# One-bank accumulator tiles and a new order at the end of a stage, in a two-block transformer kernel

## The chip, the cores and the metric

The kernel runs on one core of a Trainium2 chip. The metric is the device time of one execution in microseconds (us), as the median of three runs. The work is done by TensorE (PE; its weight loads are shown apart as PEld), VectorE (DVE), ScalarE (ACT) and GpSimd (POOL); SyncE (SP) issues most of the DMAs.

## The reference

The input is one sequence of 256 tokens with 1024 features in fp32. A first block has two layers, a second block has one. Cut to what matters here:

```python
def first_block(x, ...):                       # two layers
    for layer in range(2):
        f = swiglu(rms_norm(x, g[0]), w_ffn_gate, w_ffn_up, w_ffn_down)   # d_ff = 2816
        x = x + 0.5 * rms_norm(f, g[1])
        h = rms_norm(x, g[2])
        m = short_conv_mixer(h, ...) if layer == 0 else diff_attention(h, k, v, ...)
        x = x + rms_norm(m, g[3])
        f = swiglu(rms_norm(x, g[4]), ...)
        x = x + 0.5 * rms_norm(f, g[5])
        if layer == 0:
            k, v = shared_kv(x, g_kv, w_kv)

def second_block(x, ...):                      # one layer
    proj = rmsnorm(x, norm1_g) @ w_in
    y_a = hgrn2_mixer(...); y_b = nsa_mixer(...)
    merged = g_a * (y_a @ w_br_a) + g_b * (y_b @ w_br_b)
    h = x + merged @ w_out
    h = h + square(relu(rmsnorm(h, norm2_g) @ w_ff1)) @ w_ff2             # d_ff = 4096
    return rmsnorm(h, final_g)
```

## The kernel before

**Precision and weights.** Every large product is made of three fp32r matmuls: each operand is split into a rounded part and a remainder, and high by high, low by high and high by low are added up in PSUM. The weights are streamed from HBM in chunks of two pieces (128 x 1024 each) through three raw buffers. `Stream.hi` (L162) makes the rounded part of the next piece on ACT (L171, tile `wh`), `Stream.lo` (L175) makes its remainder on DVE (L181, tile `wl`) and then calls `load`, which issues the DMA for a further chunk on SP (L148) when a raw buffer has been used up. There are ten slots for split pieces: `hi` does nothing when the slot ten pieces back has not been given back by `done`, and nothing when the raw chunk may not be loaded yet. `pump` is one `hi` and one `lo`.

**Stages.** The 256 tokens are two blocks of 128 (`tb` 0 and 1). A stage begins with `stage_ab` (or, for the attention and for the second block, with `section`s): it multiplies block 0 and then block 1 of the normed, transposed input by the first pieces of the stage's weights. Its input is `XT`: `fill(tb)` makes eight transposes on PE into two PSUM tiles `tr` (L385), and ACT and DVE copy them out as rounded part `xth` (L389) and remainder `xtl` (L390); for one stage they lie in tiles `h` instead (L395, L396). `fill(1)` stands inside `stage_ab`, ahead of the last quarter of block 0's work.

**The end of a stage.** The kernel has eight stage ends, each a `Tail`: ends 1, 3, 4 and 6 close the four gated FFNs, end 2 the convolution, end 5 the attention's output projection, end 7 the merge of the second block's two mixers, and end 8 the last FFN and with it the kernel. `lead` adds rows 0 to n-2 of block 0; `close` adds the last row of block 0, then the rows of block 1. A row is 6 matmuls of 512 columns into two accumulators. After a block's last row comes its norm, in four steps: `c1` reads the two accumulators on ACT (squares, L287) and DVE (L309, or L303 where there is no norm on the output) and starts a root on POOL (L298); `c2` adds to the residual `x` (L320) and takes squares again; `c3a` multiplies by the next gain (L334) and starts the second root; `c3b` scales (L338). Then the block can be transposed by `fill`.

**Order.** Inside `with ordered():` the instructions of PE, ACT, DVE and POOL are each kept in the order in which they are written; outside of it a scheduler orders them. Every engine works through its own queue in that order, so an instruction that waits holds up all behind it on its engine. In `close` the splits of the next stage's pieces (`st.hi`, `st.lo`), the norm steps, the rows and `fill(0)` are interleaved by hand.

**PSUM.** There are eight banks of 512 fp32 columns. The tags `mm` and `tr` have two tiles of one bank each. The tag `acc` has two tiles of two banks each: `new_acc` gives block 0 the first bank and block 1 the second bank of each tile. The attention scores (`att_scores`, two score maps of a head) and the scores of the second block (`nsa_scores`, two branches) take one such tile, one map or branch to a bank.

Of the kernel before, what the change touches and what calls it, by code (L numbers as in the profile page):

```python
# [209 lines left out]
def tile_model(ctx: ExitStack, tc: tile.TileContext, w, wkv, x_in, gains, cst_in, pos_in, lbp, out):  # L210
# [10 lines left out]

    def ps(tag, n=512):
        uid[0] += 1
        return psum.tile([P, n], F32, name=f"{tag}_{uid[0]}", tag=tag)

# [194 lines left out]
    def new_acc():  # L420
        t = [ps("acc", D).rearrange("p (t c) -> p t c", t=2) for _ in range(2)]
        return lambda tb, n: t[n][:, tb]

# [28 lines left out]
    @contextmanager  # L452
    def ordered():
        order.mark(False)
        yield
        order.mark(True)
# [86 lines left out]
    class Tail:  # L543
# [19 lines left out]
        def close(self, at=None, ahead=0):  # L563


            bd, n = self.bd, self.n
            at = n - 1 if at is None else at
            with ordered():
                for i in range(at, n):
                    self.row(0, i)  # L570
                rows = list(range(ahead, n - 1))
                for i in rows[:2]:
                    self.row(1, i)
                st.hi()
                bd.c2(0)
                bd.c3a(0)
                st.hi()
                st.lo()
                bd.c3b(0)
                for i in rows[2:4]:  # L580
                    self.row(1, i)
                    st.hi()
                    st.lo()
                for i in rows[4:]:
                    self.row(1, i)
                    st.hi()
                st.lo()
                bd.fill(0)
                self.row(1, n - 1)
                st.hi()  # L590
                st.lo()
                bd.c2(1)
                bd.c3a(1)
                st.lo()
                bd.c3b(1)
                while st.lo():
                    pass
# [120 lines left out]
    st.load()  # L718
    g0b = [ps("acc", D)[:, :512] for _ in range(2)]
    for n in range(2):  # L720
# [117 lines left out]
    def att_scores(h, kq):  # L838
        sc = ps("acc", D).rearrange("p (c k) -> p c k", c=2)
        for c in range(2):  # L840
            r = slice(c * 64, c * 64 + 64)
            mm(sc[:, c, 0:256], kq[r, 1, P:], kq[r, 0], True, True)
            mm(sc[:, c, 256:384], kq[r, 1, :P], kq[r, 0, :P], True, True)
        return sc

    def att_soft(h, sc):
        ev = sb([P, D], "ev", bufs=2)
        dg = sc[:, :, 128:384].rearrange("p c (a k) -> p c a k", a=2)
        nc.vector.tensor_tensor(dg, dg, negm[:, None, None, :].to_broadcast([P, 2, 2, P]), op=OP.add)
        nm = sb([P, 4], "nm", bufs=2)  # L850
        p = ev[:, :768].rearrange("p (c k) -> p c k", c=2)
        sm = sb([P, 4], "sm", bufs=2)
        spans = (slice(0, 256), slice(256, 384))
        for i, sp in enumerate(spans):
            nc.vector.tensor_reduce(nm[:, 2 * i:2 * i + 2], sc[:, :, sp], axis=AX.X, op=OP.max, negate=True)
        for i, sp in enumerate(spans):
            for c in range(2):
                q = 2 * i + c
                nc.scalar.activation(p[:, c, sp], sc[:, c, sp], AF.Exp, bias=nm[:, q:q + 1], accum_out=sm[:, q:q + 1])
        r = sb([P, 4], "smr", bufs=2)  # L860
        nc.vector.reciprocal(r, sm)
        rl = sb([P, 4], "rl", bufs=2)
        nc.vector.tensor_scalar(rl, r, neglam, None, op0=OP.mult)
        at = sb([P, D], "tmp", bufs=2)
        for i, sp in enumerate(spans):
            nc.vector.tensor_scalar(p[:, 1, sp], p[:, 1, sp], rl[:, 2 * i + 1:2 * i + 2], None, op0=OP.mult)
            nc.vector.scalar_tensor_tensor(at[:, sp], p[:, 0, sp], r[:, 2 * i:2 * i + 1], p[:, 1, sp],
                                           op0=OP.mult, op1=OP.add)
        return at
# [57 lines left out]
    def acc(tb, n):  # L927
        if tb and not acc1:
            acc1.extend(ps("acc", D)[:, :512] for _ in range(2))
        return (acc0, acc1)[tb][n]  # L930
# [241 lines left out]
    def nsa_scores(i):  # L1172
# [4 lines left out]
        cs = slice(tb * P, (tb + 1) * P)  # L1177
        sc = ps("acc", D).rearrange("p (b c) -> p b c", b=2)
        for b_ in range(2):
# [142 lines left out]
    def hg_sums(tb):  # L1322
# [3 lines left out]
        mm(o2, up, af[:, tb], True, True)  # L1326
        od = ps("acc", D)
        for h in range(4):
# [19 lines left out]
    def hg_attn(tb):  # L1348
# [4 lines left out]
        for c in range(2 - tb):  # L1353
            o = hv(ps("acc", D)[:, :512])
            r = slice(c * 64, c * 64 + 64)
# [77 lines left out]
    ya_h, ya_l = sb([P, KD, T], "xth", F32R)[:, :4], sb([P, KD, T], "xtl", F32R)[:, :4]  # L1433
    ob = [ps("acc", D).rearrange("p (m t) -> p m t", m=4) for _ in range(2)]
    for m in range(KD):
        ws_piece(ob[m // 4][:, m % 4], brs[m // 2], m % 2, YX(yb_h, yb_l, 4), range(4, 8))
        nc.vector.tensor_tensor(mgs[m][:, 1], mgs[m][:, 1], ob[m // 4][:, m % 4], op=OP.mult)
    ms = []
# [153 lines left out]
```

## Time and profile before

| | |
|---|---|
| median of 3 runs | 1455.8 us (1452.35 to 1456.35) |
| the profiled execution, its own time | 1455.11 us |
| its span, first to last instruction | 1453.3 us |
| PE busy | 1411.6 us, 97% of the span |
| DVE busy, ACT busy | 884.2 us (61%), 741.5 us (51%) |
| mean granted TensorE clock | 0.996 |

The median is 0.7 us over the time of the profiled execution, which is 1.8 us over its span. The views used below are: the busy times of the engines; the table of who waited for whom; the instructions of one engine in order of time, where a bracket at the end of a row gives the idle time of the engine before that row and what ended it; the chain that ended last, in which neighbouring pieces of the same kind are merged; and the groups of instructions by line, with their shapes. A matmul's duration in these rows overlaps that of the next one; the distance between two starts is what it costs.

### The profile page before, as it was taken

Reading aid. Unit: us, or ns where it says so; the run is one execution under the profiler, and the core shown is the slowest. Engines: PE = TensorE matmul, PEld = TensorE weight load, DVE = VectorE, ACT = ScalarE, POOL = GpSimd, SP = SyncE. Lnnn points to the kernel's source line nnn. Section 1 sums busy time; section 2 is a strip of 40 time slices with the busy share of each in tenths; the row PEclk is TensorE's granted clock in tenths of the full one; section 3 lists DMA queues with packets and bytes.
Section 4 is the critical chain, followed back from the end, with each engine's and each line's share of the span. In section 5 each row is a group of like instructions: output and inputs, shape, how many; then the busy total and the mean of one; then the engine's idle time right before and its main releaser. Section 6 shows DMA issues by size and latency. Waiting matters only on the chain.

```text
span 1453.3 us, 23106 instructions
## 1 busy us (share of the span) xinstructions
PE 1411.6 (97%) x9556; PEld 1288.2 (89%) x9556; DVE 884.2 (61%) x1332; ACT 741.5 (51%) x1212; POOL 48.7 (3%) x56
## 2 busy tenths in 40 slices
PE   7999999999999999999999999999999998999997
PEld 6999979979999799998798799997887898899995
DVE  5565566866555475654776765554878556665552
ACT  5454454445444444543665554444575864464451
POOL 0000000010000000000100100000000000000000
PEclk9999999999999999999999999999999999999999
DMA  7554546446554355554343465543653233455530
GB/s 271 206 210 175 193 168 217 155 171 225 185 192 174 145 206 201 187 182 167 147 172 131 160 232 187 191 168 126 232 189 116 98 148 135 146 200 196 184 143 29
DMA packets 37801, 252.93 MB, mean 174 GB/s; under 512 B 4288, under 2 KB 4672, under 8 KB 8896
## 3 DMA queue, kind: packets, MB, share of 16 engines
q1 hardware_dynamic: 36656, 250.20, 47.4%
q8 instruction: 75, 1.23, 0.3%
q10 hardware_dynamic: 1008, 1.25, 0.2%
q14 instruction: 30, 0.25, 0.0%
q0 software_dynamic: 32, 0.00, 0.0%
HBM read 250.39 MB, written 1.05 MB: 173 GB/s over the span
## 4 chain that ended last, share of the span: by engine, by line
PE 87%; DVE 5%; DMA 2%; ACT 2%; issue 2%; POOL 1%; POOLq 0%; DVEq 0%; ACTq 0%
PE mm L399 58%; PE acc L399 25%; PE tr L399 2%; DMA raw<-in_w_dram 2%; DVE wl L181 2%; POOL ssr L298 1%; ACT junk L287 1%; ACT wh L171 1%; DVE x L320 1%; PE tr L385 1%; PE tr L521 0%; PE tr L1203 0%; DVE tmp L309 0%; DVE xtl L390 0%; DMA gain<-in_gains_dram 0%
## 5 line engine op out<-in xcount | busy, mean ns | idle before, releaser
L181 DVE TENSOR_TENSOR wl<-raw,wh 128x1024 fp32r<-128x1024 f32 (+1 forms) x460 | 550.3, 1219 | 188.6 <-ACT wh L171 185.3
L171 ACT ACTIVATE wh<-raw 128x1024 fp32r<-128x1024 f32 (+1 forms) x460 | 473.1, 1050 | 187.5 <-PE mm L399 92.8
L399 PE MATMUL mm<-xth,wh 128*128 128x256 f32 x1728 | 490.7, 284 | 3.6 <-DVE ev L1449 3.6
L399 PE MATMUL mm<-xtl,wh 128*128 128x256 f32 x1728 | 488.5, 283 | 0.0
L399 PE MATMUL mm<-xth,wl 128*128 128x256 f32 x1728 | 486.1, 281 | 0.0
L399 PE MATMUL acc<-wh,h 128*128 128x512 f32 x1120 | 354.3, 397 | 3.8 <-DVE tmp L309 3.2
L399 PEld LDWEIGHTS mm<-xth,wh 128*128 128x128 f32 x1728 | 324.2, 188 | 6.5 <-DVE ev L1449 4.2
L399 PEld LDWEIGHTS mm<-xth,wl 128*128 128x128 f32 x1728 | 327.1, 189 | 0.6 <-issue 0.5
L399 PEld LDWEIGHTS mm<-xtl,wh 128*128 128x128 f32 x1728 | 325.0, 188 | 2.1 <-issue 0.5
L399 PEld LDWEIGHTS acc<-wh,h 128*128 128x128 f32 x1120 | 205.8, 188 | 53.4 <-DVE tmp L309 5.3
L399 PE MATMUL acc<-wl,h 128*128 128x512 f32 x560 | 221.3, 395 | 0.0
L399 PE MATMUL mm<-wh,xth 128*128 128x256 f32 (+2 forms) x496 | 159.2, 321 | 7.9 <-ACT xth L389 7.9
L399 PE MATMUL mm<-wh,xtl 128*128 128x256 f32 (+2 forms) x496 | 158.3, 319 | 4.1 <-DVE xtl L390 4.0
L399 PE MATMUL mm<-wl,xth 128*128 128x256 f32 (+2 forms) x496 | 157.2, 317 | 0.0
L399 PEld LDWEIGHTS acc<-wl,h 128*128 128x128 f32 x560 | 105.2, 188 | 25.4
L527 ACT ACTIVATE ev<-mm 128x256 f32<-128x256 f32 x74 | 28.4, 384 | 166.4 <-PE mm L399 165.1
L399 PEld LDWEIGHTS mm<-wh,xth 128*128 128x128 f32 x496 | 96.0, 194 | 14.8 <-ACT xth L389 10.6
L399 PEld LDWEIGHTS mm<-wh,xtl 128*128 128x128 f32 x496 | 96.2, 194 | 10.2 <-DVE xtl L390 6.1
L399 PEld LDWEIGHTS mm<-wl,xth 128*128 128x128 f32 x496 | 96.1, 194 | 4.6
L528 DVE TENSOR_TENSOR ev<-ev,mm 128x256 f32<-128x256 f32 x74 | 31.2, 421 | 99.0 <-ACT ev L527 99.0
L427 ACT ACTIVATE h<-ev 128x256 fp32r<-128x256 f32 x114 | 47.4, 418 | 81.9 <-DVE ev L528 38.0
L428 DVE TENSOR_TENSOR h<-ev,h 128x256 fp32r<-128x256 f32 x114 | 48.2, 425 | 51.8 <-ACT h L427 51.8
(276 smaller groups left out, 960.2 us busy)
## 6 DMA issues: line engine op xcount, KB each, us to landing
raw<-in_w_dram SPq DMA_DIRECT2D x225, 1024.0 KB, 4.8
gain<-in_gains_dram SPq DMA_DIRECT2D x15, 512.0 KB, 3.8
raw<-in_wkv_dram SPq DMA_DIRECT2D x4, 792.0 KB, 4.7
x<-in_x_dram SPq DMA_DIRECT2D x2, 512.0 KB, 5.4
raw<-in_w_dram SPq DMA_DIRECT2D x2, 512.0 KB, 5.6
ev<-in_lbp_dram SPq DMA_DIRECT2D x1, 512.0 KB, 5.8
out_dram<-tmp ACTq DMA_DIRECT2D x2, 256.0 KB, 2.8
out_dram<-tmp SPq DMA_DIRECT2D x2, 256.0 KB, 2.6
```

The costliest lines, as they stand in the source:

```text
L171: self.nc.scalar.activation(h, r, AF.Copy)
L181: self.nc.vector.tensor_tensor(l, r, h.bitcast(F32), op=OP.subtract)
L287: nc.scalar.activation(junk, src, AF.Square, accum_out=self.ss[key][:, n:n + 1])
L298: nc.gpsimd.tensor_tensor(self.r[key], v[:, 1:2], half[:, :1], op=OP.pow)
L320: nc.vector.scalar_tensor_tensor(x[:, tb, c], self.t[tb][:, c], r, x[:, tb, c], op0=OP.mult, op1=OP.add)
L385: nc.tensor.transpose(pt[:, j * P:(j + 1) * P], xn[:, k * P:(k + 1) * P], ident)
L399: nc.tensor.matmul(o, lhsT=a, rhs=b, start=start, stop=stop)
L427: last["act"] = nc.scalar.activation(dst[:, 0], src, AF.Copy).ins
L428: last["dve"] = nc.vector.tensor_tensor(dst[:, 1], src, dst[:, 0].bitcast(F32), op=OP.subtract).ins
L527: nc.scalar.activation(s, o[:, 0], AF.Silu)
L528: nc.vector.tensor_tensor(hf, s, o[:, 1], op=OP.mult)
```

## The change

1. All accumulators become tiles of one bank: `ps` loses its width, and the tag `acc` gets four tiles of one bank in place of two of two banks. `new_acc` gives each of its four accumulators (2 blocks x 2 halves) a tile of its own. The tiles that used only a part of two banks (`g0b`, `acc1`, the sums of `hg_sums`, the products of `hg_attn`) shrink to one bank. The four pairs of the merge (`ob`) lie in four tiles in place of two.
2. `att_scores` gives each of the two score maps a tile of its own, and `att_soft` handles them one after the other: the mask is added in two instructions of 256 columns in place of one of 512, and the maximum is taken in four instructions (256 and 128 columns for each map) in place of two.
3. `nsa_scores` puts both branches into one bank (256 columns each), with four such tiles in flight in place of two.
4. `close` has a new order. `c3b(0)` follows `c3a(0)` directly, with no split between. Only four `hi` and two `lo` stand ahead of `fill(0)` (there were seven and four). `fill(0)` comes after the fifth of eight rows of block 1 (it came after the seventh). Two `hi` and two `lo` follow until the last row, and no split lies between that row and `c3b(1)`; what is left of `lo` comes after it. In all, six `hi` are written in place of eight.

```diff
-    def ps(tag, n=512):
+    def ps(tag):
         uid[0] += 1
-        return psum.tile([P, n], F32, name=f"{tag}_{uid[0]}", tag=tag)
+        return psum.tile([P, 512], F32, name=f"{tag}_{uid[0]}", tag=tag, bufs=4 if tag == "acc" else 2)
...
     def new_acc():
-        t = [ps("acc", D).rearrange("p (t c) -> p t c", t=2) for _ in range(2)]
-        return lambda tb, n: t[n][:, tb]
+        t = [ps("acc") for _ in range(4)]
+        return lambda tb, n: t[2 * tb + n]
...
             at = n - 1 if at is None else at
+            rows = list(range(ahead, n))
             with ordered():
                 for i in range(at, n):
                     self.row(0, i)
-                rows = list(range(ahead, n - 1))
-                for i in rows[:2]:
-                    self.row(1, i)
+                self.row(1, rows[0])
                 st.hi()
                 bd.c2(0)
                 bd.c3a(0)
-                st.hi()
+                bd.c3b(0)
+                for i in rows[1:5]:
+                    self.row(1, i)
+                    if i < rows[4]:
+                        st.hi()
                 st.lo()
-                bd.c3b(0)
-                for i in rows[2:4]:
-                    self.row(1, i)
-                    st.hi()
-                    st.lo()
-                for i in rows[4:]:
-                    self.row(1, i)
-                    st.hi()
                 st.lo()
                 bd.fill(0)
+                for i in rows[5:-1]:
+                    st.hi()
+                    self.row(1, i)
+                st.lo()
+                st.lo()
                 self.row(1, n - 1)
-                st.hi()
-                st.lo()
                 bd.c2(1)
                 bd.c3a(1)
-                st.lo()
                 bd.c3b(1)
                 while st.lo():
                     pass
...
     def att_scores(h, kq):
-        sc = ps("acc", D).rearrange("p (c k) -> p c k", c=2)
+        sc = [ps("acc") for _ in range(2)]
...
-        dg = sc[:, :, 128:384].rearrange("p c (a k) -> p c a k", a=2)
-        nc.vector.tensor_tensor(dg, dg, negm[:, None, None, :].to_broadcast([P, 2, 2, P]), op=OP.add)
+        for c in range(2):
+            dg = sc[c][:, 128:384].rearrange("p (a k) -> p a k", a=2)
+            nc.vector.tensor_tensor(dg, dg, negm[:, None, :].to_broadcast([P, 2, P]), op=OP.add)
...
-        for i, sp in enumerate(spans):
-            nc.vector.tensor_reduce(nm[:, 2 * i:2 * i + 2], sc[:, :, sp], axis=AX.X, op=OP.max, negate=True)
-        for i, sp in enumerate(spans):
-            for c in range(2):
+        for c in range(2):
+            for i, sp in enumerate(spans):
                 q = 2 * i + c
-                nc.scalar.activation(p[:, c, sp], sc[:, c, sp], AF.Exp, bias=nm[:, q:q + 1], accum_out=sm[:, q:q + 1])
+                nc.vector.tensor_reduce(nm[:, q:q + 1], sc[c][:, sp], axis=AX.X, op=OP.max, negate=True)
+            for i, sp in enumerate(spans):
+                q = 2 * i + c
+                nc.scalar.activation(p[:, c, sp], sc[c][:, sp], AF.Exp, bias=nm[:, q:q + 1], accum_out=sm[:, q:q + 1])
...
-        sc = ps("acc", D).rearrange("p (b c) -> p b c", b=2)
+        sc = ps("acc").rearrange("p (b c) -> p b c", b=2)
...
-    ob = [ps("acc", D).rearrange("p (m t) -> p m t", m=4) for _ in range(2)]
+    ob = [ps("acc").rearrange("p (m t) -> p m t", m=2) for _ in range(4)]
     for m in range(KD):
-        ws_piece(ob[m // 4][:, m % 4], brs[m // 2], m % 2, YX(yb_h, yb_l, 4), range(4, 8))
-        nc.vector.tensor_tensor(mgs[m][:, 1], mgs[m][:, 1], ob[m // 4][:, m % 4], op=OP.mult)
+        ws_piece(ob[m // 2][:, m % 2], brs[m // 2], m % 2, YX(yb_h, yb_l, 4), range(4, 8))
+        nc.vector.tensor_tensor(mgs[m][:, 1], mgs[m][:, 1], ob[m // 2][:, m % 2], op=OP.mult)
```

## Rows read from the trace of the kernel before

**Rows 1.** The page's busy times: us (share of the span) x instructions.

```profile
PE 1411.6 (97%) x9556; PEld 1288.2 (89%) x9556; DVE 884.2 (61%) x1332; ACT 741.5 (51%) x1212; POOL 48.7 (3%) x56
```

**Rows 2.** Who waited for whom, PE alone: us in total, times, longest us.

```profile
PE mm L399 <- ACT xth L389: 7.9, 5, 2.2
...
PE acc L399 <- DVE tmp L309: 3.2, 4, 0.8
PE tr L385 <- DVE tmp L338: 3.2, 4, 1.2
PE mm L399 <- DVE h L396: 1.2, 1, 1.2
```

**Rows 3.** PE in order of time at end 1: start us, us, instruction [idle before].

```profile
197.02 0.74 PE L399 MATMUL acc<-wh,h 128*128 128x512 f32 x2 [0.81 <-DVE tmp L309]
...
206.97 1.03 PE L385 MATMUL tr<-cst,tmp 128*128 128x128 f32 x8
...
211.45 0.38 PE L399 MATMUL mm<-wh,xth 128*128 128x256 f32 x1 [2.03 <-ACT xth L389]
...
222.22 1.03 PE L385 MATMUL tr<-cst,tmp 128*128 128x128 f32 x8
```

**Rows 4.** ACT in order of time at end 1.

```profile
209.85 1.06 ACT L171 ACTIVATE wh<-raw 128x1024 fp32r<-128x1024 f32 x1 [3.25 <-DMA raw<-in_w_dram]
210.81 1.07 ACT L389 ACTIVATE xth<-tr 128x512 fp32r<-128x512 f32 x2
```

**Rows 5.** DVE in order of time at end 1.

```profile
196.27 1.45 DVE L309 SCALAR_TENSOR_TENSOR tmp<-acc,gain 128x512 f32<-128x512 f32 x2 [7.59 <-ACT junk L287]
...
203.03 0.88 DVE L338 TENSOR_SCALAR tmp<-tmp,ssr 128x512 f32<-128x512 f32 x2 [0.44 <-POOL ssr L298]
...
211.43 1.29 DVE L390 TENSOR_TENSOR xtl<-tr,xth 128x512 fp32r<-128x512 f32 x2 [4.11 <-ACT xth L389]
212.63 1.28 DVE L309 SCALAR_TENSOR_TENSOR tmp<-acc,gain 128x512 f32<-128x512 f32 x2
...
220.07 0.88 DVE L338 TENSOR_SCALAR tmp<-tmp,ssr 128x512 f32<-128x512 f32 x2 [0.44 <-POOL ssr L298]
```

**Rows 6.** The chain that ended last: starts of `stage_ab` after ends 1, 2, 3, 5.

```profile
212.17 10.21 PE mm L399 x71
...
312.98 8.60 PE mm L399 x71
...
507.83 10.13 PE mm L399 x71
...
821.58 8.60 PE mm L399 x71
```

**Rows 7.** DVE in order of time at end 5.

```profile
817.43 3.49 DVE L181 TENSOR_TENSOR wl<-raw,wh 128x1024 fp32r<-128x1024 f32 x3
...
829.47 0.88 DVE L338 TENSOR_SCALAR tmp<-tmp,ssr 128x512 f32<-128x512 f32 x2 [0.44 <-POOL ssr L298]
```

**Rows 8.** PE in order of time at ends 4, 6 and 7.

```profile
717.04 1.06 PE L385 MATMUL tr<-cst,tmp 128*128 128x128 f32 x8 [1.25 <-DVE tmp L338]
...
1024.15 1.06 PE L385 MATMUL tr<-cst,tmp 128*128 128x128 f32 x8 [0.36 <-DVE tmp L338]
...
1260.47 0.38 PE L399 MATMUL mm<-wh,xtl 128*128 128x256 f32 x1 [0.34 <-DVE xtl L390]
```

**Rows 9.** PE's weight loads in order of time at end 8.

```profile
1433.49 0.30 PEld L399 LDWEIGHTS acc<-wh,h 128*128 128x128 f32 x2 [0.52 <-DVE x L303]
...
1434.82 0.30 PEld L399 LDWEIGHTS acc<-wh,h 128*128 128x128 f32 x2 [0.80 <-DVE ssv L293]
```

**Rows 10.** Groups by line and shape, DVE, 710 to 812 us: busy us, mean ns.

```profile
L849 DVE TENSOR_TENSOR acc<-acc,cst 128x512 f32<-128x512 f32 x8 | 5.6, 696 | 0.4 <-PE acc L399 0.3
L855 DVE TENSOR_REDUCE nm<-acc 128x2 f32<-128x512 f32 x8 | 5.5, 691 | 0.2
...
L855 DVE TENSOR_REDUCE nm<-acc 128x2 f32<-128x256 f32 x8 | 3.3, 416 | 0.0
```

More of the change, by code (lines that the diff above doesn't have):

```diff
@@ L718, in tile_model @@
     st.load()
-    g0b = [ps("acc", D)[:, :512] for _ in range(2)]
+    g0b = [ps("acc") for _ in range(2)]
     for n in range(2):
@@ L838, in att_scores @@
     def att_scores(h, kq):
-        sc = ps("acc", D).rearrange("p (c k) -> p c k", c=2)
+        sc = [ps("acc") for _ in range(2)]
         for c in range(2):
             r = slice(c * 64, c * 64 + 64)
-            mm(sc[:, c, 0:256], kq[r, 1, P:], kq[r, 0], True, True)
-            mm(sc[:, c, 256:384], kq[r, 1, :P], kq[r, 0, :P], True, True)
+            mm(sc[c][:, 0:256], kq[r, 1, P:], kq[r, 0], True, True)
+            mm(sc[c][:, 256:384], kq[r, 1, :P], kq[r, 0, :P], True, True)
         return sc
@@ L928, in acc @@
         if tb and not acc1:
-            acc1.extend(ps("acc", D)[:, :512] for _ in range(2))
+            acc1.extend(ps("acc") for _ in range(2))
         return (acc0, acc1)[tb][n]
@@ L1326, in hg_sums @@
         mm(o2, up, af[:, tb], True, True)
-        od = ps("acc", D)
+        od = ps("acc")
         for h in range(4):
@@ L1353, in hg_attn @@
         for c in range(2 - tb):
-            o = hv(ps("acc", D)[:, :512])
+            o = hv(ps("acc"))
             r = slice(c * 64, c * 64 + 64)
```

## The prediction, made before the changed kernel was run

> **What bounds the kernel now.** I read the busy times first. PE is busy for 97% of the span [rows 1], and its matmuls are not touched by the change, so a gain can come only from PE's idle time, 1453.3 - 1411.6 = 41.7 us, and from stretches in which PE runs at the lower clock. The table of who waited for whom says which idle time the diff can reach: 7.9 us for `xth`, 3.2 us for L309, 3.2 us for L338 and 1.2 us for L396 [rows 2], all of them norm and transpose steps at the ends of stages. The rest lies at the start of the kernel, behind its last matmul and in the merge, where the diff changes nothing of weight.
>
> End 1 shows the pattern. After block 0's last row PE sits idle for 0.81 us until L309 has read the first accumulator [rows 3], though the next row goes to the other bank of that tile. Seven rows later come the transposes of block 0 at 206.97, then the last row, and then PE waits 2.03 us for `xth` [rows 3]. ACT tells why: the transposes were long done, but ahead of `xth` in its queue stood the seventh `hi`, which waited 3.25 us for its raw chunk [rows 4]. DVE gets `xtl` only at 211.43 for the same reason, and block 1's norm behind it (L309 at 212.63, scale at 220.07) [rows 5], so that the transposes of block 1 come at 222.22 [rows 3].
>
> Then I read the first 71 matmuls of `stage_ab` in the chain: 10.21 us after end 1, 8.60 after end 2, 10.13 after end 3, 8.60 after end 5 [rows 6]. The same matmuls cost 1.6 and 1.5 us more after ends 1 and 3: PE started there at the lower of its two clock levels, behind the wait.
>
> **The change, part by part, at end 1.** I count from 196.27, the start of L309 for block 0, as t = 0 [rows 5].
>
> The false wait of 0.81 us goes: PE starts block 1's rows at t = -0.06. That the wait comes from the tile and not from the chip is also what the Trainium skill says (PSUM, Terms): engines must keep apart on a bank within a quadrant, not on neighbouring banks. The trace cannot tell the two apart by itself, since no run shows block 1's rows in a tile of their own; by the page 0.81 us can be had, and if the chip wanted the wait, nothing.
>
> A row is (206.97 - 197.02) / 7 = 1.42 us [rows 3], so five rows end at t = 6.98. Block 0's scale starts at 203.03, t = 6.76, behind POOL's root [rows 5]; I leave it there, because the `lo` that stood ahead of it ended before the root did (0.44 us idle for POOL). Half of its 0.88 us is done at t = 7.20: a new wait of 0.2 us for PE ahead of `fill(0)`. It is new because two more rows used to cover it. With three rows and the transposes (0.8 us) the stage then starts at t = 12.4. The two `xth` copies no longer stand behind a `hi` that waits for a DMA, since the first six pieces had been loaded: ACT reached the seventh before it waited. They take 1.07 us [rows 4] and end near t = 9. So the wait for `xth` is covered by the last three rows, 4.3 us.
>
> DVE's queue is the next to be late. Behind the scale (end t = 7.64) stand two `lo`, then `xtl` (1.29), then two `lo`, then `c1(1)`. A `lo` costs 3.49 / 3 = 1.16 us in a row of them [rows 7]. That gives 7.64 + 2.33 + 1.29 + 2.33 = t 13.6 for L309 of block 1, against 212.63 or t = 16.36 before. From there to its scale it was 220.07 - 212.63 = 7.44 us [rows 5], with two `lo` in it that hid in the waits for POOL; without them the chain through POOL stays, so I keep 7.44: scale at t = 21.0, its first half at 21.5. PE reaches `fill(1)` at 12.4 + 8.6 = t 21.0 and waits 0.5 us. The transposes come at t = 21.5 against 25.95 (222.22), 4.45 us earlier. Then a second new wait: the last two `lo` of the stage now stand behind `c3b(1)`, and the first is done at 21.9 + 1.16 = 23.1, while PE wants it 1.04 us (transposes and two matmuls) after 21.5, at 22.55. That costs 0.55. The second is done in time. **End 1 gains 3.9 us**, of which 1.6 are the clock. SP is moved past, too: the DMA of the chunk behind the six pieces is issued by the second `lo`, now about 1 us later, but no split needs that chunk before `stage_ab` has reached `fill(1)`, so I cost it at nothing; without that cover it would cost the 3.25 us of [rows 4].
>
> **The other ends.** End 3 has the same rows and 0.1 us less of clock: 3.8. End 2 has no clock to win: 3.9 - 1.6 = 2.3. End 4 is followed by work that needs no transposes; there I take away the wait of 1.25 us ahead of `fill(1)` [rows 8] and half of the 1.2 us for L396 [rows 2], 1.8. End 6: `fill(1)` waited 0.36 [rows 8] and the norm chain is as much earlier as at end 2, but the matmuls just ahead of that `fill(1)` need the piece whose `lo` now stands behind the scale; of 2.3 I keep 0.6. End 7 has a shorter norm, without L309; it loses a wait of 0.34 [rows 8] and small pauses: 0.6. End 8: the weight loads sat 0.52 and 0.80 us behind the reads of block 0's accumulators [rows 9]; 1.1, straight off the end.
>
> End 5 **loses**. Two of block 1's rows were done early there, so no `hi` waited for a DMA, and DVE ran without a break from its three `lo` at 817.43 to block 1's norm [rows 7]. Now four `lo` stand on that way, since the one that hid ahead of the scale is moved behind it. Block 1's scale moves from 829.47 to 830.6; PE, which ended its 71 matmuls at 821.58 + 8.60 = 830.2 just as the scale was ready, waits for it: -1.1.
>
> **The attention and the rest.** `att_soft` has three more DVE instructions a head. Rows: 512 columns cost 696 and 691 ns, 256 columns 416 [rows 10]; halving costs 2 x 416 - 696 = 136 and 2 x 416 - 691 = 141, and another 141 if the line goes on to 128 columns: 0.42 us a head, 3.3 us for eight heads. Nothing of it is on the path where PE is ahead; all of it would be if DVE were. I take 0.6, near the lower end, since the exponentials of the first map start earlier and PE's waits for DVE in this part are few. Below nothing it can go as well, by the same early start. The four tiles of `nsa_scores` and the merge I cost at zero: PE waits there for L1449, not for an accumulator.
>
> **Sum:** 3.9 + 2.3 + 3.8 + 1.8 - 1.1 + 0.6 + 0.6 + 1.1 - 0.6 = 12.4 us. Against the profiled execution (1455.1 us) that is 1442.7; the median of the runs lies 0.7 us higher, so 1443.4.
>
> **The rivals.**
> (a) *The clock and the attention take their share.* The clock stays at its lower level after two ends all the same (3.1 us back), and the attention pays its 3.3 (2.7 back): 1449.2. For it: after end 2, PE waited as long as after end 1 and kept its clock [rows 3, 6], so the wait alone doesn't decide. The Trainium skill (TensorE: Matmul & The Clock Gate, Part 1) has the lower clock as the default that activity releases; by that rule a stretch without the gap should keep the upper level, and the 3.1 us would be won.
> (b) *The change does little of what it says.* A `hi` still meets a raw chunk that has not landed, so `xth` is late as before, and the norm of block 1 with it. Then only end 8's 1.1 us, the end 4 wait and some of the false waits remain, against end 5's loss and the attention: 1455 give or take 2. Against it: six splits ran ahead of the one that waited [rows 4].
> (c) *Slower.* DVE becomes the bound at every end, as I expect of end 5. The point from which it decides is the start of block 1's L309: if it lies later than t = 16.4, `fill(1)` is later than before, and the two `lo` behind the scale (2.33 us) come on top. I have 13.6, so DVE would have to be later by 2.8 us at an end, more than two further `lo`. With 1.1 lost at end 5, 1.2 at each of four others and the attention's 3.3, less the 1.1 of end 8: about 8 us, 1464.
>
> **How the numbers follow.** Forecast 0.62, (a) 0.16, (b) 0.13, (c) 0.09. A measurement can tell about 0.3% (4.4 us) from no change, so faster holds the forecast and (a), 0.78; same is (b), 0.13; slower is (c), 0.09. For the low end I drop the two new waits at PE and the attention's cost (1.2 us at each of four ends and 0.6, with a little for the merge): 1436. At the upper end I include (a) and the better part of (b): 1452. Outside lie (c) and some of (b).
>
> **What would show it.** Right: no wait of PE for L309 at ends 1, 2, 3 and 6; no `hi` that waits for a DMA ahead of `xth`; a wait of 0.2 to 0.6 us at L385 for L338 at `fill(0)` and at `fill(1)`, and one of about half a microsecond for `wl` behind it; the 71 matmuls at 8.6 us after all ends. Wrong: waits for `xth` or `xtl` of 2 us at a stage's start, L309 of block 1 later than t = 16, a lower clock after a stage's end, or a longer attention (720 to 803 us) with PE waiting for L855 or L859.

## The result, and the profile after

The median fell from 1456.1 us (1452.4 to 1457.0, 4 runs) to 1439.4 us (1439.2 to 1440.4, 4 runs): ratio 0.990, 95% interval 0.9885 to 0.9915. The forecast was 1443.4 with a range of 1436 to 1452. The sum of the steps was 12.4 us, and 14.7 us came (1455.1 to 1440.4 us in the profiled executions). That is close, but in part by luck: ends 1 to 3 gave 6.1 us more than the steps said, and end 6 5.2 us less.

The busy times, and who PE waited for (engine, tile and line, us in total, times, the longest), of the kernel after:

```profile
PE 1406.6 (98%) x9556; PEld 1288.4 (90%) x9556; DVE 884.3 (61%) x1356; ACT 740.5 (51%) x1212; POOL 34.0 (2%) x56
...
PE mm L399 <- DVE ev L1448: 3.7, 3, 1.3
PE tr L385 <- DVE tmp L338: 3.5, 2, 2.4
PE mm L399 <- DVE wl L181: 3.5, 1, 3.5
PE mm L399 <- DVE xtl L390: 1.3, 2, 0.9
```

Against [rows 1, 2]: the 7.9 us for `xth` and the 3.2 for L309 have left the list. L338 stands at 3.5 us, but in two waits, and a wait of 3.5 us for a `lo` is new. POOL is busy for 34.0 us, with the same 56 instructions that took 48.7 before.

PE at end 1 (start, duration, instruction), for [rows 3]: the transposes of block 0, the first matmul of `stage_ab`, the transposes of block 1. The fourth row is block 1's transposes at end 3.

```profile
202.59 1.04 PE L385 MATMUL tr<-cst,tmp 128*128 128x128 f32 x8
...
207.67 0.28 PE L399 MATMUL mm<-wh,xth 128*128 128x256 f32 x1
...
216.12 1.03 PE L385 MATMUL tr<-cst,tmp 128*128 128x128 f32 x8
...
501.42 0.81 PE L385 MATMUL tr<-cst,tmp 128*128 128x128 f32 x6
```

No bracket stands behind any of them, so PE waits for nothing here. Counted from L309 of block 0, as in the prediction, the transposes of block 1 come at t = 216.12 - 195.81 = 20.31; before it was 222.22 - 196.27 = 25.95 [rows 3, 5]. From 207.67 to 216.12 there are 72 matmuls in 8.45 us; in the kernel before the last 71 of them took 10.21 [rows 6]. The granted clock from 206 to 222 us is 1.00. End 3 is the same: 501.42 - 481.12 = 20.30.

DVE at end 1, for [rows 5]:

```profile
195.81 1.45 DVE L309 SCALAR_TENSOR_TENSOR tmp<-acc,gain 128x512 f32<-128x512 f32 x2 [7.59 <-ACT junk L287]
...
201.72 0.88 DVE L338 TENSOR_SCALAR tmp<-tmp,ssr 128x512 f32<-128x512 f32 x2 [0.73 <-POOL ssr L298]
202.52 2.35 DVE L181 TENSOR_TENSOR wl<-raw,wh 128x1024 fp32r<-128x1024 f32 x2
...
208.26 1.28 DVE L309 SCALAR_TENSOR_TENSOR tmp<-acc,gain 128x512 f32<-128x512 f32 x2
...
214.01 0.88 DVE L338 TENSOR_SCALAR tmp<-tmp,ssr 128x512 f32<-128x512 f32 x2 [0.73 <-POOL ssr L298]
```

Block 0's scale starts at t = 5.91 (before 6.76), block 1's norm at 12.45 (before 16.36), its scale at 18.20; from L309 to L338 block 1 needs 5.75 us where it needed 7.44. This shortening was not in the prediction.

To see where the time went I cut the span at the first norm instruction of block 0 at each end (L309, at ends 7 and 8 L303). The us between cuts, from one profiled execution of each kernel:

| kernel | start to 1 | 1-2 | 2-3 | 3-4 | 4-5 | 5-6 | 6-7 | 7-8 | 8 to last | span |
|---|---|---|---|---|---|---|---|---|---|---|
| before | 196.3 | 100.68 | 194.89 | 199.42 | 118.70 | 190.47 | 246.17 | 186.14 | 20.56 | 1453.3 |
| after | 195.8 | 94.87 | 190.44 | 193.61 | 117.71 | 191.01 | 250.76 | 184.74 | 19.55 | 1438.5 |
| banks alone | 195.0 | 101.63 | 195.96 | 200.03 | 118.80 | 190.28 | 247.43 | 186.22 | 19.59 | 1454.9 |
| order alone | 195.3 | 96.12 | 191.55 | 194.71 | 117.55 | 190.99 | 248.34 | 185.21 | 20.52 | 1440.3 |
| before, one `hi` moved | 194.8 | 98.16 | 193.66 | 197.00 | 118.10 | 190.30 | 245.43 | 185.10 | 20.59 | 1443.1 |
| after, one `lo` put back | 195.8 | 95.65 | 191.21 | 194.40 | 117.60 | 192.44 | 246.47 | 184.74 | 19.61 | 1437.9 |
| after, again | 195.4 | 94.86 | 190.44 | 193.62 | 117.60 | 191.01 | 249.52 | 184.75 | 19.59 | 1436.8 |
| after, products beside the root | 194.9 | 95.01 | 190.76 | 193.92 | 116.97 | 192.66 | 245.70 | 184.74 | 19.56 | 1434.2 |
| end 5, two early | 195.6 | 94.87 | 190.44 | 193.61 | 120.02 | 189.00 | 249.55 | 184.74 | 20.56 | 1438.4 |
| end 5, one early | 196.0 | 94.87 | 190.43 | 193.61 | 117.59 | 189.00 | 252.21 | 184.75 | 20.46 | 1438.9 |
| end 6 in order | 194.7 | 94.86 | 190.44 | 193.62 | 117.82 | 192.37 | 244.13 | 184.74 | 19.59 | 1432.3 |
| ends 5 and 6 | 194.8 | 94.85 | 190.44 | 193.62 | 117.61 | 188.99 | 244.17 | 184.74 | 19.56 | 1428.8 |

Ends 1 to 3 gave 5.81 + 4.45 + 5.81 = 16.1 us, where 10.0 were predicted. Behind end 6, where 0.6 was to be won, 4.6 were lost. The questions were: what gave the extra 6 us, what the two halves of the change do by themselves, and what went wrong at ends 5 and 6. Each ratio below is to the kernel before on the same chip.

### The profile page after: what moved, and what is told of

Its sections match the earlier page's. It is cut to its first block, busy times and chain, and to the rows that moved or that the text cites. A ratio compares the mean times of both kernels' runs of the same rounds, so it can differ in the third digit from the quotient of the medians.

```text
span 1438.5 us, 23098 instructions
## 1 busy us (share of the span) xinstructions
PE 1406.6 (98%) x9556; PEld 1288.4 (90%) x9556; DVE 884.3 (61%) x1356; ACT 740.5 (51%) x1212; POOL 34.0 (2%) x56
## 3 DMA queue, kind: packets, MB, share of 16 engines
q8 instruction: 75, 1.23, 0.3%
q10 hardware_dynamic: 1008, 1.25, 0.3%
## 4 chain that ended last, share of the span: by engine, by line
PE 90%; DVE 5%; ACT 2%; issue 1%; DMA 1%; POOL 1%; POOLq 0%; DVEq 0%; ACTq 0%; SPq 0%
PE mm L399 58%; PE acc L399 27%; PE tr L399 2%; DVE wl L181 2%; PE tr L385 1%; ACT wh L171 1%; DVE x L320 1%; POOL ssr L298 0%; PE tr L1202 0%; PE tr L521 0%; DMA raw<-in_wkv_dram 0%; ACT junk L287 0%; DMA gain<-in_gains_dram 0%; DVE tmp L309 0%; DMA raw<-in_w_dram 0%
```

## The experiments

### The banks without the order

The kernel after with the body of `close` of the kernel before.

> The changed kernel with the old order at the end of a stage: parts 1 to 3 of the change alone. Theory (the order carries the gain, the tiles only end 8): the false wait of 0.81 us at ends 1, 2, 3 and 6 is gone, but the wait for xth grows by as much, since the seventh hi still waits for its chunk; end 8 gains 1.1. In all 1 to 3 us faster than before, 1453 to 1455. If the longer gap costs the clock at more ends, 1456 to 1458. Rival (the tiles carry the gain): 1445 or less. POOL's roots behind a lo stay at 1.40 us.

Measured: 1457.2 us against 1451.1, ratio 1.0042 (1.0027 to 1.0057). The list of who PE waited for, and ACT at end 1:

```profile
PE mm L399 <- ACT xth L389: 13.1, 6, 3.3
```

```profile
199.62 4.84 ACT L171 ACTIVATE wh<-raw 128x1024 fp32r<-128x1024 f32 x5
208.61 1.06 ACT L171 ACTIVATE wh<-raw 128x1024 fp32r<-128x1024 f32 x1 [4.15 <-DMA raw<-in_w_dram]
```

The false wait is gone (L309 has left the list), and nothing is won, except at the end of the kernel (19.59 for 20.56). PE reaches the transposes earlier, but the seventh `hi` still waits for its chunk, now 4.15 us in place of 3.25 [rows 4], and `xth` stands behind it. The wait saved comes back, with something added, at the next place. What is added is the lower clock: the first 71 matmuls of `stage_ab` take 11.10, 9.98 and 10.87 us behind ends 1, 2 and 3, where they took 10.21, 8.60 and 10.13 [rows 6]. Behind end 2 the granted clock is 0.84 (312 to 323 us) and PE's wait 3.3 us; in the kernel before it was 1.00 (314 to 325 us) behind 2.2 us. The expectation had this as its second case. So the chip does not want the false wait: a tile of its own is enough. By the Trainium skill (PSUM — Partial Sum Buffer, Terms), weighed in the prediction, engines must keep apart on a bank within a quadrant, not on neighbouring banks; the run agrees with it.

### The order without the banks

The kernel before with the body of `close` of the kernel after.

> The kernel before with the new order at the end of a stage alone, two-bank tiles and the old attention. Theory: the false wait of 0.81 us stays at ends 1, 2, 3 and 6 and 1.1 us at end 8; the rest of the gain is there: 1442 to 1445. If the attention with one-bank tiles costs its 3 us, this would be nearer to 1441. Rival (tiles and order need each other): 1450 or more. POOL's roots 0.55 us at ends 1 to 4.

Measured: 1442.2 us, ratio 0.9936 (0.9919 to 0.9953). The waits of PE:

```profile
PE tr L385 <- DVE tmp L338: 4.8, 3, 2.4
...
PE acc L399 <- DVE tmp L309: 3.2, 4, 0.8
```

The order does most of the work. The banks are worth 1.25, 1.11 and 1.10 us more at ends 1 to 3 on top of it (table, order alone less after). They are worth less than nothing alone and 3.5 us there together with the order: the two parts do not add up.

### Only the seventh `hi`

```diff
                 for i in rows[4:]:
                     self.row(1, i)
-                    st.hi()
+                    if i < rows[-1]:
+                        st.hi()
                 st.lo()
                 bd.fill(0)
+                st.hi()
```

> The kernel before with one hi moved from ahead of fill(0) to behind it, nothing else. Theory (the hi that waits for its raw chunk holds up xth): the 7.9 us of PE's waits for xth fall under 1; but that hi now stands ahead of the squares of block 1, so the transposes of block 1 are only about 1 us earlier and PE waits for L338 there instead, 1 to 2 us at each of ends 1 to 3. With the clock back after ends 1 and 3, 4 to 9 us faster than before: 1447 to 1452. Rival (xth is late because of the late scale or of the tile): no change, 1454 to 1457.

Measured: 1446.3 us, ratio 0.9966 (0.9950 to 0.9981). The waits of PE:

```profile
PE tr L385 <- DVE tmp L338: 9.2, 7, 1.9
...
PE acc L399 <- DVE tmp L309: 3.2, 4, 0.8
```

No wait for `xth` is left in the list: the `hi` that waited for its DMA was what held `xth`. Of the gain at ends 1 to 3 this one moved instruction gives 2.52, 1.23 and 2.42 us. Ends 1 and 3 get 1.2 to 1.3 us more than end 2, for the clock stays up: the windows show 1.00 behind end 1 here, and 0.84 from 212 to 223 us in the kernel before. PE then waits for the scale of block 1 instead, since its norm runs no faster.

### One `lo` put back in front of the scale

The kernel after, with one of the two `lo` ahead of `fill(0)` put back between `c3a(0)` and `c3b(0)`, where it was before.

> The changed kernel with one of the two lo ahead of fill(0) put back ahead of block 0's scale, where DVE otherwise waits for POOL. DVE does the same work. Theory (POOL's root can't proceed while DVE runs a split, and ends about 0.4 us after it): that root takes 1.40 us and not 0.55, the scale comes 0.85 us later at ends 1 to 6, and PE waits 0.2 to 0.5 us for L338 at fill(0): 1 to 3 us slower than the changed kernel, 1440 to 1442. Rival (the 1.40 us are POOL's own and come from what else is different): the root stays at 0.55, the scale at its place, and the split is free: 1438 to 1440.

Measured: 1439.7 us, ratio 0.9916 (0.9899 to 0.9932). POOL's root, and what DVE did beside it: first the kernel before (the `lo`, then the root), then this kernel, then the kernel after.

```profile
201.37 1.22 DVE L181 TENSOR_TENSOR wl<-raw,wh 128x1024 fp32r<-128x1024 f32 x1
...
201.60 1.40 POOL L298 TENSOR_TENSOR ssr<-ssv,half 128x1 f32<-128x1 f32 x1 [2.93 <-DVE ssv L296]
...
218.63 1.40 POOL L298 TENSOR_TENSOR ssr<-ssv,half 128x1 f32<-128x1 f32 x1 [2.93 <-DVE ssv L296]
```

```profile
200.89 1.22 DVE L181 TENSOR_TENSOR wl<-raw,wh 128x1024 fp32r<-128x1024 f32 x1
202.55 0.88 DVE L338 TENSOR_SCALAR tmp<-tmp,ssr 128x512 f32<-128x512 f32 x2 [0.45 <-POOL ssr L298]
...
201.12 1.40 POOL L298 TENSOR_TENSOR ssr<-ssv,half 128x1 f32<-128x1 f32 x1 [2.93 <-DVE ssv L296]
```

```profile
201.14 0.55 POOL L298 TENSOR_TENSOR ssr<-ssv,half 128x1 f32<-128x1 f32 x1 [2.93 <-DVE ssv L296]
...
213.43 0.55 POOL L298 TENSOR_TENSOR ssr<-ssv,half 128x1 f32<-128x1 f32 x1 [2.93 <-DVE ssv L296]
```

With a `lo` beside it the root takes 1.40 us and ends 0.41 us after the `lo` does (201.12 + 1.40 against 200.89 + 1.22); alone it takes 0.55. The scale starts 0.03 us behind the root's end in all three kernels, so the length is not only the profiler's. One `lo` put back moves the scale of block 0 from t = 5.91 to 6.77, and costs 0.77 to 0.79 us at each of ends 1 to 3. Half of that move is DVE's own time: the `lo` keeps DVE until t = 6.33, and only then comes the wait for the root, 0.45 us. The total still equals that of the kernel after, since the stretch behind end 6 came out shorter (246.47); that is taken up further down.

### Which instruction of DVE holds the root up

The kernel after with work added: the products of L309 for block 0 are made a second time, in the place of that `lo`.

```diff
                 bd.c3a(0)
+                if bd.ids[0] is not None:
+                    for m in range(2):
+                        c = slice(m * 512, (m + 1) * 512)
+                        nc.vector.scalar_tensor_tensor(bd.t[0][:, c], self.acc(0, m), bd.mul, bd.g[0][:, c], op0=OP.mult, op1=OP.mult)
                 bd.c3b(0)
```

> The changed kernel with work added: at each end with a post-norm (1 to 6), between the last reduction of block 0's second step and its scale, DVE makes the products of L309 again (accumulator in PSUM times gain in SBUF, two instructions of 0.69 to 0.76 us), to the same place and with the same values. They run beside POOL's root just as the one lo did that was put there before. Theory: a lo holds POOL up because both its inputs lie in SBUF; these products read one input from SBUF and one from PSUM, so the root stays at 0.55 us. Rival: any DVE instruction beside it holds the root up: then it takes about 1.4 us or more, ending 0.4 us after the product that runs as it starts. In both cases the scale of block 0 waits for DVE itself and comes at about t=6.8, so the span is 0 to 4 us above the changed kernel's.

DVE and POOL at end 1 of this kernel:

```profile
199.99 1.28 DVE L579 SCALAR_TENSOR_TENSOR tmp<-acc,gain 128x512 f32<-128x512 f32 x2
201.18 0.87 DVE L338 TENSOR_SCALAR tmp<-tmp,ssr 128x512 f32<-128x512 f32 x2
...
200.21 0.55 POOL L298 TENSOR_TENSOR ssr<-ssv,half 128x1 f32<-128x1 f32 x1 [2.93 <-DVE ssv L296]
```

The root runs entirely under the two products and takes 0.55 us. A product reads one input from PSUM and one from SBUF; a `lo` reads both (`raw` and `wh`) from SBUF. So not any work of DVE holds the root up. The scale comes at t = 6.30 (about 6.8 expected) because DVE itself is busy.

A product differs from a `lo` in its kind too, not only in its inputs. Two roots of the kernel after tell these apart, one near the start and one at end 7 (DVE, then POOL):

```profile
14.17 1.28 DVE L390 TENSOR_TENSOR xtl<-tr,xth 128x512 fp32r<-128x512 f32 x2
...
1236.52 1.28 DVE L334 TENSOR_TENSOR tmp<-x,gain 128x512 f32<-128x512 f32 x2
...
14.33 0.56 POOL L330 TENSOR_TENSOR ssr<-ssv,half 128x1 f32<-128x1 f32 x1 [7.30 <-DVE ssv L328]
...
1236.75 0.87 POOL L298 TENSOR_TENSOR ssr<-ssv,half 128x1 f32<-128x1 f32 x1 [52.87 <-DVE ssv L296]
```

L390 is a subtraction like the `lo`, but reads `tr` from PSUM, and the root beside it takes 0.56 us. L334 is a multiplication of two SBUF tiles, and the root beside it takes 0.87 us. So it is the two SBUF inputs and not the kind of instruction.

A single execution of the kernel with the products took 1436.0 us, less than the kernel after in spite of the added work; that is end 6 once more.

### End 5: two pieces split early

```diff
         wo.row(1, 0)
-        st.pump()
+        st.pump(2)
 ...
         wo.row(0, 5)
-        st.pump()
+        st.pump(2)
     wo.close(at=6, ahead=2)
```

In the kernel after, end 5 shows this (DVE, POOL, PE):

```profile
806.15 1.22 DVE L181 TENSOR_TENSOR wl<-raw,wh 128x1024 fp32r<-128x1024 f32 x1
807.28 0.15 DVE L296 SCALAR_TENSOR_TENSOR ssv<-ss,ssv 128x1 f32<-128x1 f32 x1
807.35 1.22 DVE L181 TENSOR_TENSOR wl<-raw,wh 128x1024 fp32r<-128x1024 f32 x1
...
807.57 1.40 POOL L298 TENSOR_TENSOR ssr<-ssv,half 128x1 f32<-128x1 f32 x1 [9.40 <-DVE ssv L296]
...
813.12 1.07 PE L385 MATMUL tr<-cst,tmp 128*128 128x128 f32 x8 [2.36 <-DVE tmp L338]
```

> The changed kernel as it is, once more, beside the runs that follow: they are compared with it on one chip. Expected: the span within 2 us of 1438.5, with the same waits of PE at end 5 (2.4 us at the transposes of block 1) and at end 6 (3.5 us for a lo), since both come from the order of the instructions and not from chance. If either wait is missing, or the stretch from end 6 to end 7 comes out at 246 to 248 us as with one lo put ahead of the scale of block 0, then that loss was one of a single execution.

> The changed kernel, with two hi and lo in place of one at each of the two places of the attention's last ordered block where the stream is pumped. Theory: end 5 lost 2.4 us because close's six hi only reach M+5 there, and the last two pieces were split by the request for the next four chunks, whose lo slid between the two steps of the norm of block 1 (one root at POOL 1.40 us instead of 0.55, and L309 to L338 longer by the two lo). With two pieces split earlier nothing is left to slide in: all four roots at end 5 0.55 us, the wait at the transposes of block 1 down from 2.4 to under 0.5 us, 1.5 to 2.4 us off the span. Rival: the wait stands, since block 1's norm starts too late there in any case (its 16 rows are not the cover that the other ends have), or the splits moved forward delay the attention's last copies on ACT and block 0's norm starts later by as much: then the start of the norm at end 5 moves from 792.4 to 793.5 to 795 and the span is the same within 0.5 us.

Measured in one set: the kernel after 1438.7 us (ratio 0.9897, 0.9883 to 0.9912), this kernel 1440.3 (0.9909, 0.9893 to 0.9926). The second execution of the kernel after showed both waits again (2.27 and 3.6 us) and 249.5 us from end 6 to end 7. The new kernel's wait at end 5 is 0.50 us and all four roots take 0.55 or 0.56, as the theory had it; but the rival holds too: the start of end 5 moved by 2.4 us (117.60 to 120.02). These two rows of PE tell why:

```profile
786.78 0.50 PE L399 MATMUL mm<-wh,h 128*128 128x512 f32 x1 [1.83 <-DVE h L905]
...
788.82 1.20 PE L399 MATMUL mm<-wh,h 128*128 128x512 f32 x2
```

The first of the two extra splits stands in front of the attention's last copies; PE waits 1.83 us for those (0.85 in the kernel after), and the matmuls behind the wait run slower (1.20 us for a pair that takes 0.63; the granted clock is 0.83 from 786 to 796 us). What was won at block 1's transposes was lost 26 us ahead of them.

### End 6 put in order

`bd.ids == (11, 13)` picks end 6, `(9, 10)` further down end 5.

```diff
                 st.lo()
                 st.lo()
+                if bd.ids == (11, 13):
+                    st.lo()
                 self.row(1, n - 1)
                 bd.c2(1)
+                if bd.ids == (11, 13):
+                    st.hi()
+                    st.hi()
                 bd.c3a(1)
```

In the kernel after, end 6 shows this on ACT, DVE and PE; the last row is a window of 10 us (PE, PEld, DVE, ACT and POOL busy, granted clock, DMA share, GB/s):

```profile
997.91 0.87 ACT L171 ACTIVATE wh<-raw 128x792 fp32r<-128x792 f32 x1 [2.35 <-DMA raw<-in_wkv_dram]
998.68 0.58 ACT L287 ACTIVATE junk<-acc 128x512 bf16<-128x512 f32 x1
...
999.38 0.69 DVE L309 SCALAR_TENSOR_TENSOR tmp<-acc,gain 128x512 f32<-128x512 f32 x1 [3.10 <-ACT junk L287]
...
1006.61 0.54 PE L399 MATMUL mm<-wl,xth 128*128 128x512 f32 x1 [3.50 <-DVE wl L181]
...
1000.00:1010.00 10.00, 6.50 (x27) 5.20 (x26) 8.55 (x17) 3.14 (x8) 1.25 (x3) 0.85 0.13 27
```

> The changed kernel, at end 6 alone with one more lo ahead of the last row of block 1, and two hi set down by hand behind the squares of that block's second step. Theory: end 6 lost because its closing six hi and four lo leave two 1024-column pieces whose lo stand behind the norm of block 1, and because two hi that nothing orders slid between the two squares of that norm, one of them waiting 2.35 us for its DMA. With the order set, PE's wait of 3.5 us for a lo at 1006.6 goes, the scale of block 1 is kept 2 to 3 us earlier, the clock stays at full in that stretch, and 3 to 5 us come off the span, all between end 6 and end 7 (250.8 down to 246 to 248). Rival: the wait for the lo is paid as a wait at the transposes of block 1, which come 2.6 us behind it in PE's order: then under 1.5 us is gained. Second rival: the stretch is longer for a cause behind it (attention-like work of the merge), then the wait goes and the stretch stays at 250.

Measured: 1433.7 us, ratio 0.9862 (0.9847 to 0.9876), 5.0 us under the kernel after in the same set. From end 6 to end 7 it takes 244.13 us (246 to 248 expected), 2.0 less than before the change. The same window:

```profile
1000.00:1010.00 10.00, 9.74 (x51) 8.25 (x50) 9.20 (x21) 6.63 (x12) 0.55 (x1) 1.00 0.42 137
```

PE no longer waits for that `lo`, nor for block 1's scale in its place, and the clock stays at 1.00.

### End 5 in another way, and both ends

At end 5 only the later pump is doubled, where the attention's last `h` is already made, and the other piece gets its `hi` by hand behind the squares of `c2(1)`, so that its `lo` falls behind the scale.

```diff
         wo.row(0, 5)
-        st.pump()
+        st.pump(2)
 ...
                 bd.c2(1)
+                if bd.ids == (9, 10):
+                    st.hi()
                 bd.c3a(1)
```

> The changed kernel, at end 5 alone: of the two pieces whose lo slid into the norm of block 1, one is split at the attention's last pump, behind the last h of L905 (where DVE has some 2.8 us of rows 6 and 7 of block 0 to spare and one lo already stands), the other's hi is set down by hand behind the squares of block 1's second step and its lo behind the scale. Two pieces split earlier had cost at the start of the end what they gave at its wait, since the first of them stood in front of the last h of the attention (PE's wait for it 0.9 to 1.8 us). Theory: now the start stays within 0.4 us of the changed kernel's (segment from end 4 to end 5 117.6 to 118.0), block 1's scale is kept at about t=18.1 in place of 20.05, the wait at its transposes falls from 2.4 to 0.5 us, and the span by 1.5 to 2.5 us. Rival: lo ahead of the norm delays c1(0) of end 5 by 1.2 us all the same: then the segment ending there is 118.8 or more, and under 1 us is left. Second rival: the last lo, now behind the scale, comes late for the matmuls behind the transposes: a wait for wl of up to 1.5 us in place of the old one.

> The changed kernel with both mends: end 5 as in the kernel with one piece split early, end 6 with the third lo ahead of the last row and the two hi behind the squares. Theory: the two are independent, since each lies in its own stretch: span 1436.8 less 4.5 to 5.4 for end 6 and less 1.5 to 2.5 for end 5, so 1429 to 1431; the stretch behind end 5 is free of the lower clock (0.96 to 0.97) that some executions show there behind the 2.4 us wait. Rival: the order at end 5 changes which pieces are in hand 190 us later and end 6's third lo stands for another piece: then the stretch from end 6 to end 7 is 246 or more instead of 244.

Measured in one set: 1438.1 us for end 5 alone (ratio 0.9888, 0.9872 to 0.9903) and 1430.7 us for both (0.9840, 0.9826 to 0.9853). At end 5 it went as expected: the start stays (117.59), the transposes wait 0.41 us, the stretch to end 6 takes 189.00 in place of 191.01. But end 5 alone gave nothing in total, because end 6 got worse by as much (252.21):

```profile
996.41 0.87 ACT L171 ACTIVATE wh<-raw 128x792 fp32r<-128x792 f32 x1 [2.82 <-DMA raw<-in_wkv_dram]
...
PE mm L399 <- DVE wl L181: 4.0, 1, 4.0
```

The unordered `hi` between the squares waited 2.82 us for its DMA there, 2.35 in the kernel after: the norm came earlier, the chunk did not. With end 6 in order the gain stays, and the list of waits of the best version is:

```profile
PE acc L399 <- DMA gain<-in_gains_dram: 6.7, 1, 6.7
PE mm L399 <- DVE ev L1455: 3.7, 3, 1.3
PE tr L385 <- DVE tmp L338: 1.7, 2, 1.2
```

This version is 1.6% faster than the kernel before, where the change alone is 1.0% faster, and the two intervals lie apart (0.9826 to 0.9853 and 0.9883 to 0.9912, in two sets).

## Why the prediction was right, point by point

**What bounds the kernel: right.** PE's busy time fell by 5.0 us (1411.6 to 1406.6), its idle time by 14.8 - 5.0 = 9.8. The first part is in the main the lower clock behind ends 1 and 3: 72 matmuls take 8.45 us, where 71 of them took 10.21 and 10.13.

**Ends 1 to 3: right in mechanism, the terms too small.** 10.0 us were predicted, 16.1 came. The false wait went, the `hi` that waited went, the clock stayed up, as the steps said. The step that failed is the one about POOL: "I leave it there, because the `lo` that stood ahead of it ended before the root did (0.44 us idle for POOL)" and "without them the chain through POOL stays, so I keep 7.44". The root ended after the `lo` because of the `lo`. Without one beside it the root is 0.85 us shorter, once in block 0's chain (scale at t = 5.91, not 6.76) and twice in block 1's (5.75 us, not 7.44). The two new waits of PE (0.2 and 0.5 us) and the one for `wl` (0.55) then did not come: block 1's transposes came at t = 20.31 instead of 21.5, and PE got there without a pause. Transposes 1.19 us earlier and a wait of 0.55 us that did not come make 1.7 of the 2 us that each end gave beyond its step. For block 0's chain the run with the `lo` put back shows it (0.77 to 0.79 us an end); for the two of block 1 it is read from the rows at ends 1 to 3, and only at end 5 did runs take two `lo` out of block 1's norm.

Two sums of the prediction are off by about 0.1 us: five rows of 1.42 from t = -0.06 end at 7.04, not 6.98, and 7.20 + 0.8 + three rows is 12.26, not 12.4. Neither moves its t = 21.5, which the scale sets.

In before's rows the sign of this could be seen: [rows 5] shows "0.44" idle for POOL ahead of each scale, and the root rows of POOL, which the prediction didn't read, have two lengths, 0.55 and 1.40. An "idle, waiting for POOL" asks for POOL's own row.

Split by the runs, ends 1 to 3 gained: the `hi` moved, 2.5 / 1.2 / 2.4; the rest of the order, 2.0 / 2.1 / 2.3; the banks on top, 1.25 / 1.1 / 1.1.

**End 4 and the attention: the sum right, its parts not.** 1.8 - 0.6 = 1.2 was predicted for the stretch from end 4 to end 5, and 0.99 came. The order alone gives 1.15 there; the attention's three added instructions a head cost 0.05 to 0.16 us (order alone against the two executions of the kernel after), near the lower end of their bound of 0 to 3.3.

**End 5: a loss, as predicted, by another way.** PE waits 2.36 us (1.1 predicted) and 0.5 us of the stretch are lost. Not the four `lo` on the way made it, but two further ones that `close` does not order: the request for the next chunks pumps twice, and the scheduler put both `lo` into the gaps of block 1's norm, beside its root. With the same wait, the kernel with end 6 in order lost 1.4 us more in that stretch (192.37 for 191.01). A window of 25 us behind the wait, of the kernel after and of that kernel:

```profile
815.00:840.00 25.00, 25.00 (x213) 25.00 (x212) 18.80 (x22) 15.14 (x20) 0.00 (x0) 1.00 0.60 216
```

```profile
815.00:840.00 25.00, 25.00 (x206) 25.00 (x206) 16.53 (x19) 13.96 (x19) 0.00 (x0) 0.97 0.57 211
```

PE is busy throughout in both, but does fewer matmuls at the lower clock. The kernels with the `lo` put back and with the products show the same (0.93 and 0.96 in that window, 192.44 and 192.66 us). Why one execution keeps its clock behind this wait and another does not stays open.

**End 6: wrong.** 0.6 was to be won; 4.6 and, in the second execution, 3.4 us were lost. The step said that the piece's `lo` "now stands behind the scale" and kept 0.6 of 2.3 for it. That `lo` cost 3.5 us of waiting, because two `hi` outside of the order slid into block 1's norm, the one that waited for its DMA between its two squares. That delayed the norm by 3 us, the scale with it, and the `lo` behind the scale. Where those `hi` stand is the scheduler's choice: with the products added it set them behind both squares, and the stretch took 245.7 us. The lower clock took the rest, 0.85 around the wait and 0.83 again from 1090 to 1100 us. The second execution of the kernel after had 1.00 in the latter stretch and lost 1.2 us less. With the order set by hand both are gone.

**Ends 7 and 8: right in sign, end 7 too small.** End 7 gave 1.40 us where 0.6 was predicted; the one `hi` moved gives 1.04 of it by itself (186.14 to 185.10). End 8 gave 1.01 (1.1). The two kernels mended at end 5 alone show 20.56 and 20.46 there, but their last multiplication starts 14.96 us behind the cut as in the kernel after (15.94 before); it is the output's DMAs that take 0.9 us longer to land.

**The rivals.** (a) does not hold: the clock stays up behind ends 1 and 3 (1.00 from 206 to 222 and from 492 to 508 us), and the attention costs next to nothing. (b) does not hold for the whole change, but for the banks alone it is what happened: 1457, no gain. (c) names the mechanism of ends 5 and 6, where DVE became late; at ends 1 to 3 it was early.

## What to carry to other kernels

A wait removed may be worth nothing until the next one behind it is covered as well: the single-bank tiles alone made this kernel 0.4% slower, the same tiles with the new order 1% faster. Where a chain goes through POOL, read POOL's own rows, with what DVE runs beside them, and keep two-input SBUF work of DVE out of those gaps. Instructions that the hand-written order leaves out are set down by the scheduler in the gaps of the chain that the order protects; put every split that can fall there into the order.

## What the runs showed of the hardware that was not expected

A root of 128x1 elements on POOL took 0.55 us beside an idle DVE or beside a product with one PSUM input, and 1.40 us when a subtraction with both inputs in SBUF had started 0.23 us earlier. It then ended 0.41 us after that subtraction, in the kernel before as in the one with the `lo` put back. The Trainium skill (SBUF — State Buffer, SBUF: two separate sides, and Who interferes with whom) states that a DVE instruction with two SBUF inputs contends with a GpSimd instruction that reads SBUF, that whoever starts first holds the shared port pair for the whole instruction, and that a DVE instruction with at most one SBUF input, outside the 2-port perf modes, does not contend. The runs agree: 1.40 with the `lo`, 0.87 with L334, 0.55 with the product, 0.56 with L390, 0.55 alone. The 0.41 us left behind the subtraction are less than the 0.55 of a whole root, so a part of the root was not held up; which part, no run shows.

The lower of TensorE's two clock levels (1.2 of 2.4 GHz; a granted clock between 0.5 and 1 in a window is a mixture) stood behind waits of PE of 2.0 and 2.1 us at ends 1 and 3 before (0.84), of 3.3 us at end 2 with the banks alone (0.84) and of 3.5 us at end 6 (0.85). It did not stand behind 2.2 us at end 2 before (1.00). Behind the waits of 2.3 to 2.4 us at end 5 the 25 us from 815 show 1.00 in both executions of the kernel after and 0.93 to 0.97 in three other kernels with the same wait (the `lo` put back, the products, end 6 in order). From 1090 to 1100 us in the kernel after it stood at 0.83 with PE busy throughout and no wait over 0.4 us in the 50 us ahead. So the length of a wait is not the whole rule. With both ends mended the mean was 0.998, before the change 0.996.
